# Hybrid decoder layer on one core: the array steps of the state-space heads in three runs per pair, TensorE in the order of the trace, stored halves loaded one pair ahead

## The chip, the cores and the metric

The kernel runs on one core of a Trainium2 chip. The core has five engines that work side by side: TensorE (PE in the profile; PEld is its weight load), VectorE (DVE), ScalarE (ACT), GpSimd (POOL) and SyncE (SP), whose queue issues this kernel's DMAs. The metric is the device time of one execution in microseconds; lower is better. It is 1691.22 us before the change, the median of three runs.

## The reference

One layer of a hybrid decoder, float32, a sequence of 2048 positions, width 1024. The input is normalised and multiplied by one wide matrix; the result feeds two head groups. Group A is a chunked state-space scan with 16 heads of 64, in chunks of 128 positions; group B is a short gated convolution. Both are joined and projected back, normalised, and added to the input. Then a 256-wide embedding is projected, gated and added. Cut to what matters here:

```python
xbc, dt_raw, z_ssd, sc_h, sc_b, sc_c, z_sc = split(rmsnorm(x) @ w_in)
...
# group A, per chunk of 128 positions and per head
cb = einsum("bclgn,bcsgn->bgcls", cc, bc)
y_diag = einsum("bgrcls,bcsgrp->bclgrp", cb[:, :, None] * decay_in, xd)        # outputs
states = einsum("bclgn,bclgrp->bcgrpn", bc, xd * decay_states[..., None])       # states
y_off = einsum("bclgn,bcgrpn->bclgrp", cc, prev_states) * decay_out[..., None]  # offsets
y = y_diag + y_off + d_skip * x
y_ssd = rmsnorm(y * silu(z_ssd))                 # per group of 8 heads
# group B
y_sc = sc_b * causal_dwconv(sc_c * sc_h) * silu(z_sc)
mix = concatenate([y_ssd, y_sc]) @ w_out
x = x + rmsnorm(mix)
return x + sigmoid(x @ w_ple_gate) * (p @ w_ple_proj)
```

## The kernel before

All large products run as three passes of a split type (each operand is cut into a rounded part and a remainder), 128x128 weights against 512 columns at a time. The layer has three stages.

The first stage multiplies the input with the wide matrix (lines 238 to 320, 354 to 750) and writes what the heads need to memory: the convolved values `xs_d`, the gates `gz_d`, the two shared operands `cb_d`, and the running sums of the decay `acs_d`; group B's result goes to `ysc_d`.

The second stage, lines 814 to 1045, is the one that is edited. It handles the sequence in two blocks of 1024 positions (`TB`), each in 8 chunks of 128, and in each block four *pairs*. A pair is two tiles of 128 channels, `j` and `j + 4`, its two *halves* (`gr` 0 and 1), each with two heads (`hh`). That makes eight pairs. Each is written as a set of functions, its *steps*:

- `xs0`, `xs1` (`loads`, L887): the DMA of a half's values into a buffer `xs`; three of these are in use in turn.
- `T0`, `T1` (`transposes`, L891): eight transposes on TensorE into PSUM (`px`), which VectorE scales into `xd` (L903) and `xdd` (L904).
- `load0`, `load1`: DMAs that broadcast decays, `ea` (L911) and the four masks `m` (L946). `decays` (L914) takes the exponent of `ea`; `m00` to `m11` (L948) do so for the masks and multiply them with a shared operand on VectorE (L954).
- `gz0`, `gz1` (L916): the DMA of a half's gates.
- `states` (L920): 32 matmuls `pst` in the profile, a chain of 14 or 16 short operations on VectorE (L938), and two multiplications of `ea` (L941).
- `offsets` (L956): 64 small matmuls `py` (L967) for both halves.
- `out0`, `out1` (`outputs`, L971): 32 matmuls `py` each (L979), then on VectorE the skip and the gate (L982, L983), the store to `yz_d` (L984), the square on ScalarE (L988) and its sum `ssum` (L989). The store reads the buffer that `loads` had filled.

After each block `norms` (L1002) forms the norm of group A from `ssum`: four matmuls `pn` (L226) and a chain through memory. `gs` are two steps at the start of a block (`pg` L867, `pb` L879).

TensorE would have little to do in these steps. The rest of its time goes to the *filler* `under` (L819): the part of the output projection that needs group B alone, 768 matmuls `os` (L838) in 256 *units* of three. Its results go to `part_d`. A list `steps` is written out by hand (L1019 to L1034), and the loop behind it (L1039) runs a step and then as many units as that step's share of the list gives, 22 of them ahead. The list has 127 steps. Near its end the filler also starts `mixes`, which load `yz_d` or `ysc_d` and split it into operands (L792) for the later groups.

This order is only the order in which instructions are traced. The framework then orders each engine's instructions itself, by a priority that follows the trace and by its own estimate of when an operand will be there. On TensorE it so draws filler units ahead of steps, and cuts steps in two. Within an engine the resulting order is fixed; what an instruction has to wait for is a semaphore. A tile's buffer is given to the next tile of its tag when all readers of the old one are done. PSUM has three buffers of two banks for the steps (`pss`) and two banks for the filler (`psm`).

The third stage (L1048 on) does the rest of the output projection, `mo` (called through L210), which adds `part` to it (L1072) to give `x`; then norm, residual, and the gate product `mg`. `out_proj(0)` handles the first two groups of 512 positions, `out_proj(2)` the others. `Loads` (L758) hands out buffers, three per pool; `begin` issues a DMA and `get` returns the tile, after `begin` where that has not been called.

Of the kernel before, what the change touches and what calls it, by code (L numbers as in the profile page):

```python
# [7 lines left out]
F32 = mybir.dt.float32  # L8
# [7 lines left out]
P = 128  # L16
D = 1024
T = 2048
KD = D // P
KM = 2 * KD  # L20
TB = 1024
# [36 lines left out]
def hybrid_kernel(ctx: ExitStack, tc: tile.TileContext, xT, pT, w_t, w_dt, w_o, w_g, w_p, cols_d, cst_d, outT):  # L58
# [47 lines left out]
    class Weights:  # L106
# [4 lines left out]
        def __init__(self, seq):  # L111
            self.seq, self.n, self.ready = seq, 0, []
# [240 lines left out]
    with ExitStack() as st:  # L353
# [373 lines left out]
        for b, prs, order in groups:  # L727
# [16 lines left out]
            if b + 1 < NB:  # L744
# [5 lines left out]
                if n in (6, 7, 8, 9, 10):  # L750
                    next(prep, None)

    pss = ctx.enter_context(tc.tile_pool(name="pss", bufs=3, space=PSUM))
# [58 lines left out]
    with ExitStack() as st:  # L814
# [32 lines left out]
        def heads(b):  # L847
# [34 lines left out]
            def pair(j):  # L882
# [2 lines left out]
                xd, xdd, xs, gz, st = [None, None], [None, None], [None, None], [None, None], {}  # L885

                def loads(gr):  # L887
                    xs[gr] = t4.tile([P, TB], F32, tag="xs", name=f"xs_{b}{jts[gr]}", bufs=3)
                    nc.sync.dma_start(xs[gr], xs_d[b][jts[gr]])

                def transposes(gr):  # L891
                    jt = jts[gr]
                    px = flat(pss.tile([P, 2, TG], F32, tag="ssd", name=f"px_{b}{jt}"))
                    for c in range(NCH):
                        cs = slice(c * CH, (c + 1) * CH)
                        TE.transpose(px[:, cs], xs[gr][:, cs], ident)
                    xd[gr] = t4.tile([P, NCH, P], F32, tag="xd", name=f"xd_{b}{jt}", bufs=3)
                    xdd[gr] = t4.tile([P, NCH, P], F32, tag="xdd", name=f"xdd_{b}{jt}")

                    def bc(a):  # L900
                        return a[:, 2 * jt:2 * jt + 2, :].rearrange("p h c -> p c h").unsqueeze(3).to_broadcast([P, NCH, 2, 64])
                    r4 = lambda a: a.rearrange("p c (h q) -> p c h q", h=2)
                    V.tensor_tensor(r4(xd[gr]), px.rearrange("p (c h q) -> p c h q", c=NCH, h=2), bc(dts[b]), ALU.mult)  # L903
                    V.tensor_tensor(r4(xdd[gr]), r4(xd[gr]), bc(dst[b]), ALU.mult)  # L904
# [106 lines left out]
        for b in range(NB):  # L1011
# [5 lines left out]
        NJ = len(pairs) // NB  # L1017
        both = lambda *fs: lambda: [f() for f in fs]
        p = pairs[0]  # L1019
        steps += [both(begins[0], p["xs0"], p["xs1"], p["load0"], p["load1"]), gs[0][0], gs[0][1], p["T0"],  # L1020
                  both(p["gz0"], p["gz1"]), p["decays"], p["T1"], no, p["m00"], no]
        for n, p in enumerate(pairs):
            b, j = divmod(n, NJ)
            q = pairs[n + 1] if n + 1 < len(pairs) else dict.fromkeys(p, no)
            fresh = j == NJ - 1 and b + 1 < NB
            steps += [both(p["states"], q["xs0"]), p["m01"], p["m10"], p["m11"], p["offsets"], p["out0"]]
            steps += [both(q["load0"], begins[b + 1]) if fresh else q["load0"], q["T0"], both(q["decays"], q["xs1"])]
            if fresh:

                steps += [p["out1"], q["load1"], norms[b], gs[b + 1][0], gs[b + 1][1], both(q["T1"], q["gz0"], q["gz1"]), no,  # L1030
                          q["m00"], no]
            else:
                steps += [p["out1"], both(q["load1"], q["gz0"]), both(q["T1"], q["gz1"]), q["m00"], no]
        steps += [norms[-1]]  # L1034

        filler = under()
        units, lead = 0, 22
# [7 lines left out]
            pass  # L1045


    with ExitStack() as st:  # L1048
        pp = st.enter_context(tc.tile_pool(name="pp", bufs=2))
        L3 = Loads(st, "pl3", 3)  # L1050

        x2s_, ssq_, rs_, sp_ = {}, {}, {}, {}

        def out_proj(t):

            for tg in (t, t + 1):
                x2s_[tg] = [None] * KD
                ssq_[tg] = pp.tile([P, TG], F32, tag="ssq", name=f"ssq2_{tg}")
            for dp in range(0, KD, 2):
                sp = []  # L1060
                for tg in (t, t + 1):
                    x2, ssq = x2s_[tg], ssq_[tg]
                    ps = pss.tile([P, 2, TG], F32, tag="ssd", name=f"mo_{tg}_{dp}")
                    pt = L3.get("part", tg, dp)
                    for i in range(2):
                        for q in range(2):
                            if tg == t:
                                sp.append(W.next(len(sp)))
                            mm3([(ps[:, i, :], sp[2 * i + q], acts_o[tg])], 4 * q, 4, KD)
                        d = dp + i  # L1070
                        x2[d] = pp.tile([P, TG], F32, tag="x2", name=f"x2_{tg}_{d}", bufs=NG * KD)
                        V.tensor_tensor(x2[d], ps[:, i, :], pt[:, i, :], ALU.add)  # L1072
                        if d == 0:
                            S.activation(ssq, x2[d], AF.Square)
                        else:
                            sq = pp.tile([P, TG], F32, tag="sq2", name=f"sq2_{tg}_{d}")
                            S.activation(sq, x2[d], AF.Square)
                            V.tensor_tensor(ssq, ssq, sq, ALU.add)
                        yield

        def norm(tg):

            ps = mm_bank(f"pn2_{tg}")
            TE.matmul(ps, ones_d, ssq_[tg], start=True, stop=True)
            rs = rs_[tg] = pp.tile([P, TG], F32, tag="rs2", name=f"rs2_{tg}")
            S.activation(rs, ps, AF.Sqrt, bias=epsc[:, 0:1])
            V.reciprocal(rs, rs)

        def residual(tg, d):

            x2, xk = x2s_[tg], L3.get("xres", tg, d)
            for i in range(2):
                V.scalar_tensor_tensor(x2[d + i], x2[d + i], col(C_POST + d + i), rs_[tg], ALU.mult, ALU.mult)
                V.tensor_tensor(x2[d + i], x2[d + i], xk[:, i, :], ALU.add)

        def operands(tg, d):

            for i in range(2):
                sp_.setdefault(tg, []).append(split_act(x2s_[tg][d + i], f"x2s_{tg}_{d + i}", FIRST[2 * (tg % 2) + d // 4]))

        def gate(t):

            for dp in range(0, KD, 2):
                sp = []
                for tg in (t, t + 1):
                    banks = pss.tile([P, 2, TG], F32, tag="ssd", name=f"mg_{tg}_{dp}")
                    for i in range(2):
                        d, ts_, ps = dp + i, slice(tg * TG, (tg + 1) * TG), banks[:, i, :]
                        pe = pp.tile([P, TG], F32, tag="pe", name=f"pe_{tg}_{d}")
                        nc.sync.dma_start(pe, ple_d[tg * TG // TB][d, :, tg * TG % TB:tg * TG % TB + TG])  # L1110
                        for q in range(2):
                            if tg == t:
                                sp.append(W.next(len(sp)))
                            mm3([(ps, sp[2 * i + q], sp_[tg])], 4 * q, 4, KD)
                        th = pp.tile([P, TG], F32, tag="gth", name=f"gth_{tg}_{d}")
                        S.activation(th, ps, AF.Tanh, scale=0.5)  # L1116
                        V.scalar_tensor_tensor(th, th, 1.0, pe, ALU.add, ALU.mult)  # L1117
                        V.scalar_tensor_tensor(th, th, 0.5, x2s_[tg][d], ALU.mult, ALU.add)
                        nc.sync.dma_start(outT[d, :, ts_], th)
                        yield  # L1120


        plan = {}

        def after(unit, *steps):
            plan.setdefault(unit, []).extend(steps)

        def second(tg, at_norm, at_res, at_ops):

            after(at_norm, lambda: norm(tg))  # L1130
            for n, u in enumerate(at_res):
                after(u - 1, lambda d=2 * n: L3.begin("xres", tg, d))
                after(u, lambda d=2 * n: residual(tg, d))
            for n, u in enumerate(at_ops):
                after(u, lambda d=2 * n: operands(tg, d))

        def mixes_at(tg, *units):
            m = mixes(tg, 0)
            for n, u in enumerate(units):
                after(u, *m[2 * n:2 * n + 2])  # L1140

        mixes_at(1, -1, -1, 0, 1)
        mixes_at(2, 12, 13, 14, 14)
        mixes_at(3, 15, 15, 16, 17)
        second(0, 16, (19, 20, 21, 22), (29, 29, 30, 30))
        second(1, 18, (24, 25, 26, 27), (31, 31, 32, 32))
        second(2, 32, (35, 36, 37, 38), (45, 45, 46, 46))
        second(3, 34, (40, 41, 42, 43), (47, 47, 48, 48))
        for step in plan.get(-1, ()):
            step()  # L1150
        u = 0
        for stage in (out_proj, gate):
            for t in range(0, NG, 2):
                for _ in stage(t):
                    for step in plan.get(u, ()):
                        step()
                    u += 1
# [62 lines left out]
```

## Time and profile before

| what | us |
|---|---|
| runs | 1688.46, 1693.49, 1691.22 |
| median | 1691.22 |
| the profiled execution's own time | 1696.51 |
| its span, first to last instruction | 1694.8 |
| mean granted clock of TensorE | 0.994 |
| second stage, first to last `os` | 1032.5 to 1318 |
| DMA's share of the second stage's pairs | 0.73 to 0.90 |

Times in the views count from the first instruction. In a row of the timeline stand the start, the length, the engine, the line, the operation, output and inputs by name, the shape and the number of instructions merged; in brackets is the engine's idle time before the row and what ended it. Rows of TensorE overlap a little, as matmuls are pipelined: a duration per matmul is best taken from the starts of two rows. In a row of the waits stand the total, the number of times and the longest. In a row of the groups stand the busy time, the mean in ns of one instruction, and the engine's idle time ahead of them.

### The profile page before, as it was taken

What the parts mean: (1) busy time and instruction counts of PE and PEld (TensorE: products, weight loads), DVE (VectorE), ACT (ScalarE), POOL (GpSimd) and SP (SyncE); (2) the same over time, 40 slices, a digit from 0 to 9 for tenths busy, and PEclk for the clock granted to TensorE, in tenths of its full rate; (3) what the DMA queues carried; (4) which work ended last, traced back from release to release, by engine and by line L of the source; (5) the groups of instructions that cost most, each with busy time, mean ns of one, the idle gap of its engine ahead of it and who ended that gap; (6) DMA issues with size and microseconds to landing.
All of it is one profiled execution on the core that took longest, in us unless ns stands there. A gap on an engine that the chain in (4) does not pass through costs nothing.

```text
span 1694.8 us, 22689 instructions
## 1 busy us (share of the span) xinstructions
PE 1665.9 (98%) x8368; PEld 1360.3 (80%) x8368; DVE 1248.1 (74%) x1837; ACT 780.4 (46%) x1402; POOL 44.8 (3%) x79
## 2 busy tenths in 40 slices
PE   9999999999999999999999999999999899999998
PEld 7888888888888888888888888787777677788886
DVE  6998778988679867778776685779587748878632
ACT  7763544434348434344444364646565324252421
POOL 0000000000000100000000000000000000000000
PEclk9999999999999999999999999999999999999999
DMA  8452322862227322121222248789787735636422
GB/s 299 155 193 81 103 93 89 265 225 106 70 69 248 108 74 100 59 88 67 106 102 83 69 146 267 233 257 293 240 298 229 244 100 168 195 103 211 148 95 87
DMA packets 121539, 261.22 MB, mean 154 GB/s; under 512 B 16970, under 2 KB 18506, under 8 KB 120404
## 3 DMA queue, kind: packets, MB, share of 16 engines
q1 hardware_dynamic: 121428, 259.78, 46.2%
q8 instruction: 65, 1.06, 0.3%
q14 instruction: 46, 0.38, 0.1%
HBM read 191.40 MB, written 68.33 MB: 153 GB/s over the span
## 4 chain that ended last, share of the span: by engine, by line
PE 88%; DMA 4%; DVE 4%; issue 2%; ACT 1%; SPq 0%; POOL 0%; DVEq 0%; POOLq 0%; ACTq 0%
PE mg L210 10%; PE mo L210 8%; PE os L838 6%; PE A_ple L210 3%; PE A_xs1X L306 1%; PE A_gc6X L306 1%; PE A_gc0X L306 1%; PE A_gc7X L306 1%; PE A_gb5X L306 1%; PE A_gb6X L306 1%; PE A_gb2X L306 1%; PE A_z1X L306 1%; PE A_z3X L306 1%; PE A_gc5X L306 1%; PE A_z2X L306 1%
## 5 line engine op out<-in xcount | busy, mean ns | idle before, releaser
L838 PE MATMUL os<-act_m,ws_os 128*128 128x512 f32 x768 | 187.8, 399 | 1.6 <-ACT po L842 0.9
L210 PE MATMUL mo<-act_m,ws_o 128*128 128x512 f32 x768 | 180.8, 396 | 4.5 <-DVE x L1072 4.5
L210 PEld LDWEIGHTS mo<-act_m,ws_o 128*128 128x128 f32 x768 | 144.1, 189 | 42.0 <-issue 6.9
L210 PE MATMUL mg<-act_x2s,ws_g 128*128 128x512 f32 x768 | 176.7, 392 | 0.7 <-ACT gth L1116 0.7
L838 PEld LDWEIGHTS os<-act_m,ws_os 128*128 128x128 f32 x768 | 142.6, 190 | 37.4 <-issue 6.6
L210 PEld LDWEIGHTS mg<-act_x2s,ws_g 128*128 128x128 f32 x768 | 143.1, 188 | 34.1 <-ACT gth L1116 4.4
L135 DVE TENSOR_TENSOR ws_A_gb<-wr_A_gb,ws_A_gb 128x512 fp32r<-128x512 f32 x96 | 65.9, 686 | 34.2 <-ACT ws_A_gb L134 34.2
L134 ACT CAST ws_A_gc<-wr_A_gc 128x512 fp32r<-128x512 f32 x96 | 59.8, 623 | 59.2 <-PE A_gc5X L306 8.3
L134 ACT CAST ws_A_gb<-wr_A_gb 128x512 fp32r<-128x512 f32 x96 | 59.6, 621 | 54.6 <-PE A_gb5Z L306 4.3
L617 DVE SCALAR_TENSOR_TENSOR xo<-ux,cols,xo 128x1024 f32<-128x1024 f32 x60 | 76.6, 1280 | 5.7 <-ACT xo L613 4.6
L951 ACT ACTIVATE m<-m,adt 128x128 f32<-128x128 f32 x256 | 77.4, 392 | 1.6 <-DMA m<-acs_d 1.5
L135 DVE TENSOR_TENSOR ws_A_gc<-wr_A_gc,ws_A_gc 128x512 fp32r<-128x512 f32 x96 | 66.0, 687 | 14.6 <-ACT ws_A_gc L134 13.2
L1117 DVE SCALAR_TENSOR_TENSOR gth<-gth,pe 128x512 f32<-128x512 f32 x32 | 22.1, 690 | 70.4 <-ACT gth L1116 70.3
L1116 ACT ACTIVATE gth<-mg 128x512 f32<-128x512 f32 x32 | 19.1, 598 | 103.7 <-PE mg L210 103.6
L954 DVE SCALAR_TENSOR_TENSOR m<-m,gsb 128x1024 f32<-128x1024 f32 x32 | 39.6, 1246 | 20.4 <-ACT m L951 18.0
L199 ACT CAST act_m<-mraw 128x512 fp32r<-128x512 f32 x64 | 38.0, 620 | 30.3 <-DVE mraw L797 15.4
L210 PE MATMUL A_ple<-act_p,ws_p 128*128 128x512 f32 x192 | 48.1, 408 | 1.9 <-ACT act_p L199 1.5
L134 ACT CAST ws_A_z<-wr_A_z 128x512 fp32r<-128x512 f32 x48 | 29.9, 623 | 42.9 <-DVE wr_A_z L183 11.7
L134 ACT CAST ws_A_xs<-wr_A_xs 128x512 fp32r<-128x512 f32 x48 | 29.9, 623 | 42.5 <-issue 11.6
L135 DVE TENSOR_TENSOR ws_A_z<-wr_A_z,ws_A_z 128x512 fp32r<-128x512 f32 x48 | 32.9, 686 | 21.2 <-ACT ws_A_z L134 21.2
L210 PEld LDWEIGHTS A_ple<-act_p,ws_p 128*128 128x128 f32 x192 | 36.6, 194 | 11.9 <-ACT act_p L199 2.5
L1072 DVE TENSOR_TENSOR x<-mo,part 128x512 f32<-128x512 f32 x32 | 21.9, 684 | 29.0 <-PE mo L210 27.6
(505 smaller groups left out, 3599.8 us busy)
## 6 DMA issues: line engine op xcount, KB each, us to landing
wr_A_gc<-in_w_t_dram SPq DMA_DIRECT2D x64, 256.0 KB, 2.6
wr_A_gb<-in_w_t_dram SPq DMA_DIRECT2D x64, 256.0 KB, 2.7
m<-acs_d SPq DMA_DIRECT2D x32, 512.0 KB, 7.2
ple_d<-A_pe SPq DMA_DIRECT2D x32, 256.0 KB, 3.5
wr_A_xs<-in_w_t_dram SPq DMA_DIRECT2D x32, 256.0 KB, 3.6
ysc_d<-vs SPq DMA_DIRECT2D x16, 512.0 KB, 2.6
wr_A_z<-in_w_t_dram SPq DMA_DIRECT2D x32, 256.0 KB, 2.9
xs_d<-xo SPq DMA_DIRECT2D x16, 512.0 KB, 3.2
```

The costliest lines, as they stand in the source:

```text
L134: S.copy(sp[:, 0, :kn, :], raw[:, :kn, :])
L135: V.tensor_tensor(sp[:, 1, :kn, :], raw[:, :kn, :], sp[:, 0, :kn, :].bitcast(F32), ALU.subtract)
L199: S.copy(a[:, 0, :], src)
L210: TE.matmul(out, sp[:, a, (k0 + k) % 4, :], act[k0 + k][:, b, :], start=k0 + k == 0 and q == 0, stop=k0 + k == n - 1 and q == 2)
L306: TE.matmul(out, sp[:, a, k % 4, :], t[:, b, ts_], start=p in OPENS and k == 0 and q == 0, stop=k == nk - 1 and q == 2, skip_group_check=True)
L617: V.scalar_tensor_tensor(o, u[:, q:q + TB], col(w0 + q), o, ALU.mult, ALU.add)
L838: TE.matmul(ps, sp[:, a, k, :], acts_o[tg][KD + kk][:, b_, :], start=kk == 0 and n == 0, stop=kk == KD - 1 and n == 2)
L951: S.activation(m[:, c, :], m[:, c, :], AF.Exp, bias=nacs[b][:, h, c:c + 1])
L954: V.scalar_tensor_tensor(mf, mf, 1.0, s["gsb"][gr], ALU.min, ALU.mult)
L1072: V.tensor_tensor(x2[d], ps[:, i, :], pt[:, i, :], ALU.add)
L1116: S.activation(th, ps, AF.Tanh, scale=0.5)
L1117: V.scalar_tensor_tensor(th, th, 1.0, pe, ALU.add, ALU.mult)
```

## The change

Five edits. TensorE is wrapped from the start of the second stage to its end: each of its instructions gets an ordering edge on the one traced before, which adds no semaphore but holds the framework to the order of the trace. The list of steps is written anew, with 117 steps: a pair's TensorE work now stands in three steps, `states`, then `offsets` with both outputs, then both transposes of the next pair; an empty step stands ahead of the second of them. Both loads of the next pair's `xs` are in the `states` step. `xs` has four buffers in place of three, and `xd` two in place of three. At the list's end two more empty steps stand ahead of the last norm. In `out_proj(0)` the `part` tile of the next product is loaded one product ahead.

```diff
+    class InOrder:
+        def __init__(self, engine):
+            self.engine, self.last = engine, None
+        def __getattr__(self, name):
+            f = getattr(self.engine, name)
+            def call(*a, **k):
+                inst = f(*a, **k)
+                if self.last is not None:
+                    tc.add_manual_dep(inst.ins, self.last.ins.name, NOSYNC, reason="in the order of the trace")
+                self.last = inst
+                return inst
+            return call
+    TE = InOrder(TE)
...
-                    xs[gr] = t4.tile([P, TB], F32, tag="xs", name=f"xs_{b}{jts[gr]}", bufs=3)
+                    xs[gr] = t4.tile([P, TB], F32, tag="xs", name=f"xs_{b}{jts[gr]}", bufs=4)
...
-                    xd[gr] = t4.tile([P, NCH, P], F32, tag="xd", name=f"xd_{b}{jt}", bufs=3)
+                    xd[gr] = t4.tile([P, NCH, P], F32, tag="xd", name=f"xd_{b}{jt}")
...
-        steps += [both(begins[0], p["xs0"], p["xs1"], p["load0"], p["load1"]), gs[0][0], gs[0][1], p["T0"],
-                  both(p["gz0"], p["gz1"]), p["decays"], p["T1"], no, p["m00"], no]
+        steps += [both(begins[0], p["xs0"], p["xs1"], p["load0"], p["load1"]), gs[0][0], gs[0][1], both(p["T0"], p["T1"]),
+                  both(p["gz0"], p["gz1"]), p["decays"], p["m00"], no]
         for n, p in enumerate(pairs):
...
-            steps += [both(p["states"], q["xs0"]), p["m01"], p["m10"], p["m11"], p["offsets"], p["out0"]]
-            steps += [both(q["load0"], begins[b + 1]) if fresh else q["load0"], q["T0"], both(q["decays"], q["xs1"])]
+            steps += [both(p["states"], q["xs0"], q["xs1"]), p["m01"], p["m10"], p["m11"], no,
+                      both(p["offsets"], p["out0"], p["out1"]), both(q["load0"], begins[b + 1]) if fresh else q["load0"],
+                      both(q["T0"], q["T1"], q["decays"])]
             if fresh:
-                steps += [p["out1"], q["load1"], norms[b], gs[b + 1][0], gs[b + 1][1], both(q["T1"], q["gz0"], q["gz1"]), no,
-                          q["m00"], no]
+                steps += [q["load1"], norms[b], no, gs[b + 1][0], gs[b + 1][1], both(q["gz0"], q["gz1"]), q["m00"]]
             else:
-                steps += [p["out1"], both(q["load1"], q["gz0"]), both(q["T1"], q["gz1"]), q["m00"], no]
-        steps += [norms[-1]]
+                steps += [both(q["load1"], q["gz0"]), q["gz1"], q["m00"], no, no]
+        steps += [no, no, norms[-1]]
...
+    TE = nc.tensor
...
                     pt = L3.get("part", tg, dp)
+                    if t == 0:
+                        L3.begin("part", *((t + 1, dp) if tg == t else (t, dp + 2) if dp < KD - 2 else (t + 2, 0)))
...
+        L3.begin("part", 0, 0)
         mixes_at(1, -1, -1, 0, 1)
```

`q` is the next pair, `fresh` the last pair of the first block, and `no` an empty step.

## The prediction

> **What bounds the kernel now.** The page comes first: engines, then the waits of TensorE (PE) in order of their total.
>
> ```profile
> PE 1665.9 (98%) x8368; PEld 1360.3 (80%) x8368; DVE 1248.1 (74%) x1837; ACT 780.4 (46%) x1402; POOL 44.8 (3%) x79
> ```
> ```profile
> PE pn L226 <- DVE ssum L989: 6.4, 3, 3.6
> PE px L896 <- DMA xs<-xs_d: 6.1, 3, 2.7
> PE mo L210 <- DVE x L1072: 4.5, 4, 2.2
> ```
>
> PE is busy for 98% of the span, so a gain has to come out of its idle time or out of what it does slowly while busy. The first two waits lie in the stage of the heads, the stage that the change edits; the third lies behind it. The timeline of PE in that stage shows where they fall and what surrounds them:
>
> ```profile
> 1229.87 1.07 PE L896 MATMUL px<-cst,xs 128*128 128x128 f32 x8 [2.53 <-DMA xs<-xs_d]
> 1262.14 1.06 PE L896 MATMUL px<-cst,xs 128*128 128x128 f32 x8 [0.82 <-DMA xs<-xs_d]
> 1295.58 1.84 PE L896 MATMUL px<-cst,xs 128*128 128x128 f32 x8 [2.73 <-DMA xs<-xs_d]
> ...
> 1187.41 1.05 PE L226 MATMUL pn<-ssum,ones_d 128*32 128x512 f32 x4 [1.85 <-DVE ssum L989]
> ...
> 1317.17 0.96 PE L838 MATMUL os<-act_m,ws_os 128*128 128x512 f32 x3
> 1321.70 1.05 PE L226 MATMUL pn<-ssum,ones_d 128*32 128x512 f32 x4 [3.56 <-DVE ssum L989]
> ...
> 1325.09 1.92 PE L226 MATMUL pn<-ssum,ones_d 128*32 128x512 f32 x4 [1.03 <-DVE ssum L989]
> ```
>
> Eight transposes took 1.06 at one place and 1.84 at another. The windows view tells why; a row has the stretch and its length, the busy time of PE, its weight loads, VectorE (DVE), ScalarE (ACT) and GpSimd, then the granted clock, the DMA share and GB/s:
>
> ```profile
> 1182.00:1190.00 8.00, 6.15 (x27) 4.04 (x26) 2.13 (x3) 6.11 (x13) 0.00 (x0) 1.00 0.90 305
> 1230.80:1234.30 3.50, 3.50 (x11) 2.56 (x10) 3.30 (x4) 3.50 (x11) 0.00 (x0) 0.51 1.00 375
> 1295.60:1299.10 3.50, 3.50 (x13) 2.65 (x14) 2.32 (x3) 3.50 (x11) 0.00 (x0) 0.52 1.01 358
> 1322.60:1330.00 7.40, 6.37 (x17) 3.25 (x16) 6.17 (x10) 2.68 (x4) 0.00 (x0) 0.54 0.59 194
> ```
>
> After the idle times of 2.53, 2.73 and 3.56 us the clock was about half for 3.5, 3.5 and 7.4 us; after the 1.85 us at 1187 it stayed at 1.00. A long wait is therefore paid for again: (1 - 0.51) x 3.5 + (1 - 0.52) x 3.5 = 3.4 us for the loads, (1 - 0.54) x 7.4 = 3.4 us for the norm. The Trainium skill, "TensorE: Matmul & The Clock Gate", section "Why this matters for your kernels", asks only that idle gaps of over some 3 us be avoided; by it the two waits of 2.53 and 2.73 us would have cost no clock, and the sum below would be 3.4 us smaller. The rows show half clock behind both, so the measurement decides.
>
> **What the change removes.** (a) *Loads of xs.* At present a pair's second half is loaded into one of three buffers, and SyncE's queue stands until the store of an older half has landed:
>
> ```profile
> SPq L889 <- DMA yz_d<-xs: 32.3, 11, 6.7
> ```
>
> With four buffers and both loads issued at the states step of the pair before, each load takes the buffer of a pair whose stores are long gone. This also frees what stood behind it on the same queue: yz stores, mask loads, gate loads. The loads then have a whole pair before them. The px waits go: 6.1 us, and 3.4 us of clock. Cutting xd from three buffers to two costs nothing, as the new T0 and T1 come behind both outputs that read the old pair.
>
> (b) *The last norm.* PE had one unit of filler (x3, a k-step of "os") left between the last outputs and the norm. In the new list ten steps lie between them, and a step is followed by 234/116 = 2.02 units (117 steps instead of 127, 22 of the 256 units ahead). The price of a matmul of 128x512 comes from an undisturbed stretch, start to start:
>
> ```profile
> 1026.26 2.88 PE L306 MATMUL A_gc7X<-act_A,ws_A_gc 128*128 128x512 f32 x12
> 1028.98 2.88 PE L306 MATMUL A_gb7X<-act_A,ws_A_gb 128*128 128x512 f32 x12
> ```
>
> That is 2.72/12 = 0.227 us, 0.68 us a unit, so about 20 units or 13.7 us cover the norm's input. At present the sums needed from the end of the outputs at about 1317.2 until about 1325.1, 7.9 us. The cover is long enough: 3.56 + 1.03 = 4.6 us and 3.4 us of clock go. If it were not, they would stay.
>
> (c) *Visits to the array.* PE leaves the filler for the small matmuls and comes back; here is how one pair's steps are split:
>
> ```profile
> 1093.64 0.43 PE L924 MATMUL pst<-xdd,btok 128*64 128x128 f32 x2
> 1094.01 2.79 PE L838 MATMUL os<-act_m,ws_os 128*128 128x512 f32 x11
> 1096.72 1.96 PE L924 MATMUL pst<-xdd,btok 128*64 128x128 f32 x30
> 1098.61 5.73 PE L838 MATMUL os<-act_m,ws_os 128*128 128x512 f32 x24
> 1104.28 0.44 PE L967 MATMUL py<-ea,sprev 64*64 64x128 f32 x4
> 1104.64 0.96 PE L838 MATMUL os<-act_m,ws_os 128*128 128x512 f32 x3
> 1105.53 1.96 PE L967 MATMUL py<-ea,sprev 64*64 64x128 f32 x60
> 1107.43 1.97 PE L979 MATMUL py<-m,xd 128*64 128x128 f32 x32
> ...
> 1109.66 1.03 PE L896 MATMUL px<-cst,xs 128*128 128x128 f32 x8
> 1110.45 3.01 PE L838 MATMUL os<-act_m,ws_os 128*128 128x512 f32 x12
> 1113.39 1.97 PE L979 MATMUL py<-m,xd 128*64 128x128 f32 x32
> ```
>
> From 1104.28 to 1107.43 are 3.15 us for 64 offsets and 3 fillers. Sixty offsets took 1.90, so 64 take 2.03; the fillers take 0.68; 0.44 us is the price of one visit more. For the split states it is 0.37 + 2.71 - 2 x 0.063 - 11 x 0.227 = 0.46 us. The second output's own visit shows 2.94 - 12 x 0.227 = 0.22 us on its way in, and I put it at 0.3. Now a pair has up to three visits beyond those of the new order: states split in two in 7 of 8 pairs, offsets split in all 8, the second output apart in 7. With PE held to the order of the trace and the outputs put together, 15 x 0.45 + 7 x 0.3 = 8.8 us go; by the cheapest row 22 x 0.22 = 4.8, by the dearest 22 x 0.46 = 10.1.
>
> Removed in sum: 6.1 + 3.4 + 4.6 + 3.4 + 8.8 = 26.3 us. I count nothing for the wait of 1.85 us at the middle norm, since PE comes there only four steps and two transposes after the outputs (8 units, 5.5 us, and 1.6 us), less than the 7.9 us above; it may go or grow to some 4. I count nothing for the earlier "part" loads: the 4.5 us of "mo" wait for DVE, not for a load by name, and of them only this one lies well inside the half of "mo" that the edit touches:
>
> ```profile
> 1357.87 55.99 PE L210 MATMUL mo<-act_m,ws_o 128*128 128x512 f32 x242 [1.23 <-DVE x L1072]
> ```
>
> At most these 1.2 us could go; the number of loads on SyncE's queue stays the same.
>
> **What it adds.** PE can no longer draw filler ahead of a step that is not ready, so every late input is now idle PE, with all the filler queued behind it. Three steps matter; the DVE durations are from the groups of 1065 to 1320 us:
>
> ```profile
> L954 DVE SCALAR_TENSOR_TENSOR m<-m,gsb 128x1024 f32<-128x1024 f32 x30 | 37.2, 1248 | 19.9 <-ACT m L951 17.5 <-POOL gsb L872 1.3 <-issue 0.9
> L938 DVE SCALAR_TENSOR_TENSOR sprev<-sprev,ea,pst 128x64 f32<-128x64 f32 x112 | 22.2, 274 | 4.9 <-issue 4.0 <-PE pst L924 0.9
> L982 DVE SCALAR_TENSOR_TENSOR xs<-xs,ds,py 128x1024 f32<-128x1024 f32 x16 | 20.4, 1277 | 17.2 <-PE py L979 17.1
> L941 DVE SCALAR_TENSOR_TENSOR ea<-ct,ea 128x1024 f32<-128x1024 f32 x16 | 18.8, 1218 | 0.0
> L983 DVE TENSOR_TENSOR xs<-xs,gz 128x1024 f32<-128x1024 f32 x15 | 18.3, 1218 | 0.1
> L903 DVE TENSOR_TENSOR xd<-px,dts 128x1024 f32<-128x1024 f32 x14 | 17.1, 1219 | 3.5 <-PE px L896 3.4
> L904 DVE TENSOR_TENSOR xdd<-xd,dst 128x1024 f32<-128x1024 f32 x14 | 17.1, 1218 | 0.1
> ...
> L989 DVE TENSOR_TENSOR ssum<-ssum,gz 128x1024 f32<-128x1024 f32 x10 | 12.2, 1222 | 9.6 <-ACT gz L988 9.5
> ```
>
> *States* wait for both halves' xd and xdd. From the first output's end to the states step lie 1.9 us of the second output, 4 units, two rows of transposes of 0.8 (1109.66 to 1110.45), and 12 units: about 14.4 us. DVE has in it two times L982, L983, L989 (1.28 + 1.22 + 1.22) and four tensor products of 1.22, together 12.3 us, and perhaps a mask (1.25) and a weight split. It just fits. *Offsets* wait for 14 or 16 steps of L938 (2.8 to 3.2 us) and two of L941 (2.4), 5.5 us, before them 10 units, 6.9 us; one interposed mask still fits. *Transposes* wait for a PSUM buffer freed by L982; covered by 4 units. So an ordinary pair waits about nothing. But DVE is nearly full in the two stretches in which the mixing operands for the later groups are made as well:
>
> ```profile
> 1127.80:1160.40 32.60, 32.60 (x271) 26.29 (x270) 28.97 (x46) 22.15 (x53) 0.20 (x1) 1.00 0.84 268
> 1160.40:1200.60 40.20, 37.52 (x316) 28.58 (x315) 30.00 (x45) 27.03 (x64) 2.75 (x3) 1.00 0.90 297
> ```
>
> PE's own time for a new pair is 13 x 2.02 units (17.9 us), 1.6 of transposes, 1.9 of states, 2.0 of offsets, 3.8 of outputs and about 0.9 of visits, 28.1 us; DVE's 28.97 us in the first of these rows is more. I take 5 us of new waits for the whole stage (bounds 0, if DVE's order suits, and 20, at 2.5 us a pair).
>
> *The start of "mo".* The operands of the first group are split into buffers that "os" frees at unit 240 of 256, which in the new list comes behind the last outputs; 16 units and the norm, 12 us, are then left until "mo" asks for them. At present all but the one unit at 1317 runs ahead of those outputs, and the waits of the norm give more time still. DVE has the outputs' sums (7.4 us) and 16 operations of about 0.7 us in that time and in the 5 us in which "mo" takes them one by one. 3 us, between 0 and 8.
>
> Behind this, "mo" and "mg" keep PE busy to the end, so what the heads gain reaches the end: 26.3 - 5 - 3 = 18.3 us. The profiled execution took 1696.5 us (span 1694.8), which becomes 1678.2; it was 5.3 us above the median of the runs, 1691.2, so the forecast for the median is **1673**.
>
> **Rivals.**
> *1. DVE sets the pace.* Each pair waits 1 us more than I counted and "mo" takes its full 8 us: 18.3 - 8 - 5 = 5.3 us are left, 1686. For it speak the two DVE rows just shown; against it that DVE waits in the same groups, 17.1 us for PE's outputs and 17.5 for ScalarE's masks.
> *2. Slower: the order turns late operands into long idle times.* The place is the states step. If DVE puts the sums (L989, which wait for ScalarE) or the masks ahead of xdd, xdd comes 2.5 us late; by the rows at 1230 and 1295 such an idle time costs 1.7 us of clock more, 4.2 us a pair, 33.6 us in all against 26.3 removed: 1698.5. It decides from about 3.3 us a pair on. Against it stands that this needs the same lateness in all eight pairs. The Trainium skill, same page, section "Part 3: Packing small matmuls", has matmuls start and end strictly in their order, so that nothing behind a late one can pass it; no row quoted here shows it otherwise.
> *3. No new waits.* SyncE's queue, freed of its 32.3 us, brings masks and gates earlier, nothing waits: 26.3 us, with the middle norm and one "mo" wait up to 29.4: 1662 to 1665.
> That the edit does nothing is hardly possible: four buffers and the new list change the program whatever the order.
>
> **How the numbers follow.** A measurement of this kernel tells about 0.3% (5 us) from no change. Forecast 0.52 (1666 to 1681), rival 1 0.18, rival 2 0.10, rival 3 0.20. Rival 1 lies across the border at 1686.1, 0.08 of it faster and 0.10 the same; hence faster 0.80, same 0.10, slower 0.10. The range goes from 1660, below rival 3, to 1690, the greater part of rival 1; beyond it are rival 2 and the rest of rival 1.
>
> **What would show it.** Right: no px wait for DMA xs; one row each of x32 pst, x64 py L967, x64 L979 and x16 px per pair; no pn wait at the end; clock 1.00 from 1040 us to the end of the heads; the heads some 20 us shorter. Wrong: new PE waits on pst for xdd, on py for ea or m of over 2.5 us with clock near 0.5 behind them, or "mo" waiting for act_m by more than 8 us; or DVE busy over 95% of a pair's window.

## The result and the profile after

The changed kernel takes 1679.16 us (median of 6 runs, 1675.72 to 1683.07) where the kernel before takes 1691.76 (6 runs): ratio 0.9923, 95% interval 0.9901 to 0.9945, 12.6 us less. The forecast was 1673 in a range from 1660 to 1690. The profiled execution took 1683.07 us, its span is 1681.2 against 1694.8. Two of the twelve runs of one version below, edges and loads together on the old list, were in a slower state and are left out of its time.

The timeline of TensorE after the change, one pair in the middle and the end of the heads (in this kernel all matmuls of the heads stand under L763, the wrapper's line):

```profile
1092.09 1.97 PE L763 MATMUL pst<-xdd,btok 128*64 128x128 f32 x32
1093.99 7.09 PE L763 MATMUL os<-act_m,ws_os 128*128 128x512 f32 x30
1101.01 1.98 PE L763 MATMUL py<-ea,sprev 64*64 64x128 f32 x64
1102.92 3.71 PE L763 MATMUL py<-m,xd 128*64 128x128 f32 x64
1106.56 3.02 PE L763 MATMUL os<-act_m,ws_os 128*128 128x512 f32 x12
1109.42 1.91 PE L763 MATMUL px<-cst,xs 128*128 128x128 f32 x16
...
1293.46 13.90 PE L763 MATMUL os<-act_m,ws_os 128*128 128x512 f32 x60
1307.29 1.07 PE L763 MATMUL pn<-ssum,ones_d 128*32 128x512 f32 x8
...
1309.78 5.61 PE L210 MATMUL mo<-act_m,ws_o 128*128 128x512 f32 x24
```

States, offsets, both outputs and both transposes are one row each; in other pairs a row is split only where TensorE waited inside it. Before, the same work was cut into seven to nine rows in each pair but the last. In the heads TensorE has 118 rows before and 77 after, and it leaves the filler for a step 41 times before and 31 after. Twenty units of filler (x60) stand ahead of the last norm, and nothing waits there. The waits of TensorE after:

```profile
PE pst L763 <- DVE xdd L924: 3.7, 3, 2.4
PE mo L210 <- DVE x L1096: 3.5, 4, 1.3
PE os L763 <- ACT po L862: 2.4, 2, 1.8
PE py L763 <- DVE m L974: 2.4, 1, 2.4
...
PE mo L210 <- ACT act_m L199: 1.8, 1, 1.8
PE py L763 <- DVE ea L961: 1.2, 3, 0.4
...
PE mo L210 <- DVE act_m L200: 0.8, 1, 0.8
```

Both waits that the change was read to remove are gone: px for the loads (6.1 us) and pn for the norm (6.4 us, the middle norm's 1.85 among them). New ones stand in their place. The longer of them in the timeline, and the granted clock behind them (third figure from the end of a row of the windows view):

```profile
1164.22 2.76 PE L763 MATMUL py<-m,xd 128*64 128x128 f32 x30 [2.35 <-DVE m L974]
...
1247.23 0.41 PE L763 MATMUL pst<-xdd,btok 128*64 128x128 f32 x2 [1.12 <-DVE xdd L924]
1250.01 3.25 PE L763 MATMUL pst<-xdd,btok 128*64 128x128 f32 x30 [2.37 <-DVE xdd L924]
...
1317.14 0.50 PE L210 MATMUL mo<-act_m,ws_o 128*128 128x512 f32 x1 [1.75 <-ACT act_m L199]
```
```profile
1165.20:1168.60 3.40, 3.40 (x21) 2.78 (x17) 3.40 (x4) 2.10 (x3) 0.00 (x0) 0.51 0.86 194
1250.50:1253.90 3.40, 3.40 (x28) 2.98 (x25) 3.07 (x7) 3.40 (x13) 0.00 (x0) 0.50 1.04 423
1318.80:1322.20 3.40, 3.40 (x9) 2.19 (x7) 2.72 (x5) 1.32 (x2) 0.00 (x0) 0.51 0.54 161
```

Each of the three is followed by 3.4 us at half clock, about 1.7 us more; between the third and its stretch lies one more wait, of 0.78 us. So the heads, from the first os to the row from which mo runs on (1326.94 before, 1309.78 after), went from 294.4 to 277.4 us, 17.0 less; mo and what follows went from 367.9 to 371.4, 3.5 more, of which 0.7 are three matmuls of mo that stood between the norm's rows before.

### The profile page after: what moved, and what is told of

Its sections match the earlier page's. It is cut to its first block, busy times and chain, and to the rows that moved or that the text cites. A ratio compares the mean times of both kernels' runs of the same rounds, so it can differ in the third digit from the quotient of the medians.

```text
span 1681.2 us, 22694 instructions
## 1 busy us (share of the span) xinstructions
PE 1655.4 (98%) x8368; PEld 1358.9 (81%) x8368; DVE 1247.7 (74%) x1837; ACT 779.9 (46%) x1402; POOL 49.0 (3%) x79
## 4 chain that ended last, share of the span: by engine, by line
PE 86%; DMA 6%; DVE 4%; ACT 2%; issue 1%; SPq 1%; DVEq 0%; ACTq 0%
PE mg L210 10%; PE mo L210 8%; PE os L763 4%; PE A_ple L210 3%; DMA mraw<-yz_d 2%; PE py L763 1%; DMA ea<-acs_d 1%; PE A_xs1X L306 1%; PE A_gc6X L306 1%; PE A_gc0X L306 1%; PE A_gb5X L306 1%; PE A_gc7X L306 1%; PE A_gb6X L306 1%; PE A_z3X L306 1%; PE A_xs3X L306 1%; PE A_gc5X L306 1%
## 5 line engine op out<-in xcount | busy, mean ns | idle before, releaser
L763 PE MATMUL os<-act_m,ws_os 128*128 128x512 f32 x768 | 184.8, 396 | 3.1 <-ACT po L862 2.4
L763 PEld LDWEIGHTS os<-act_m,ws_os 128*128 128x128 f32 x768 | 142.5, 189 | 37.8 <-issue 4.7
L135 DVE TENSOR_TENSOR ws_A_gc<-wr_A_gc,ws_A_gc 128x512 fp32r<-128x512 f32 x96 | 66.1, 688 | 14.6 <-ACT ws_A_gc L134 13.3
L974 DVE SCALAR_TENSOR_TENSOR m<-m,gsb 128x1024 f32<-128x1024 f32 x32 | 39.1, 1247 | 16.3 <-ACT m L971 14.6
L134 ACT CAST ws_A_z<-wr_A_z 128x512 fp32r<-128x512 f32 x48 | 29.9, 622 | 42.7 <-DVE wr_A_z L183 10.8
L200 DVE TENSOR_TENSOR act_m<-mraw,act_m 128x512 fp32r<-128x512 f32 x64 | 41.7, 685 | 6.7 <-ACT act_m L199 6.6
```

The source lines that it names most:

```text
L134: S.copy(sp[:, 0, :kn, :], raw[:, :kn, :])
L135: V.tensor_tensor(sp[:, 1, :kn, :], raw[:, :kn, :], sp[:, 0, :kn, :].bitcast(F32), ALU.subtract)
L200: V.tensor_tensor(a[:, 1, :], src, a[:, 0, :].bitcast(F32), ALU.subtract)
L763: inst = f(*a, **k)
L974: V.scalar_tensor_tensor(mf, mf, 1.0, s["gsb"][gr], ALU.min, ALU.mult)
```

## The experiments

Ratios are to the kernel before, timed beside each version, with 95% intervals. The first three take the change apart.

**The loads alone**, on the old list and with the framework free to order:

```diff
-                    xs[gr] = t4.tile([P, TB], F32, tag="xs", name=f"xs_{b}{jts[gr]}", bufs=3)
+                    xs[gr] = t4.tile([P, TB], F32, tag="xs", name=f"xs_{b}{jts[gr]}", bufs=4)
...
-                    xd[gr] = t4.tile([P, NCH, P], F32, tag="xd", name=f"xd_{b}{jt}", bufs=3)
+                    xd[gr] = t4.tile([P, NCH, P], F32, tag="xd", name=f"xd_{b}{jt}")
...
-            steps += [both(p["states"], q["xs0"]), p["m01"], p["m10"], p["m11"], p["offsets"], p["out0"]]
-            steps += [both(q["load0"], begins[b + 1]) if fresh else q["load0"], q["T0"], both(q["decays"], q["xs1"])]
+            steps += [both(p["states"], q["xs0"], q["xs1"]), p["m01"], p["m10"], p["m11"], p["offsets"], p["out0"]]
+            steps += [both(q["load0"], begins[b + 1]) if fresh else q["load0"], q["T0"], q["decays"]]
```

> The kernel before with the loads alone changed: four xs buffers, two xd buffers, both loads of the next pair in the states step; old list, framework free to order. Theory (three separate sources: loads 9.5 us, last norm 8 us, visits 9 us, less new waits): the px waits on DMA xs (6.1 us) and the half clock behind two of them (3.4 us) go, pn waits of 6.4 us and the split visits stay (about 118 runs of one kind on TensorE in the heads); 9.5 us faster than before, some 1682. Rival A (the loads carry it all, order and list are idle): 12 to 13 us faster, 1679. Rival B (order and list carry it, loads were hidden): within 3 us of before.

1687.47 us, ratio 0.9976 (0.9962 to 0.999): 4 us, less than half of 9.5. No px wait on a load is left and only 0.7 us of pn, but one wait of 6.6 us stands in a new place. First VectorE, then TensorE, both from this kernel's timeline:

```profile
1234.60 1.28 DVE L982 SCALAR_TENSOR_TENSOR xs<-xs,ds,py 128x1024 f32<-128x1024 f32 x1 [0.94 <-PE py L979]
1244.70 0.75 DVE L797 SCALAR_TENSOR_TENSOR mraw<-mraw,cols,gn 128x512 f32<-128x512 f32 x1 [8.82 <-DMA mraw<-yz_d]
```
```profile
1257.72 3.25 PE L924 MATMUL pst<-xdd,btok 128*64 128x128 f32 x30 [6.58 <-DVE xdd L904]
```

VectorE stood 8.8 us for the load of a mixing operand (L797) that is needed only some 70 us later at mo. The framework had drawn it ahead of the pair's own gates and xdd: its place in the list is unit 240 of the filler's 256 or later, and 197 had run. Behind it all of these came late. The clock was half from 1253.6 to 1260.4; 4.1 us of this lie in the wait itself, so it cost 1.3 us more. Rival A falls by the time. Rival B's 3 us lie within the interval (1.7 to 6.4 us); it falls by the trace, as the px waits of 6.1 us are gone. The theory's sum falls twice: this wait and its clock took 7.9 us back, and 5.7 us of pn waits that were to stay went, as 30 matmuls of filler now stood between the last outputs and the last norm.

**The list without the ordering edges**, that is the changed kernel less the wrapper:

```diff
-    TE = InOrder(TE)
```

> The changed kernel without the ordering edges on TensorE; list, loads and part tiles as changed. Theory: the framework draws filler ahead again, so visits come back (about 9 us) and the filler before the last norm is used up early (pn waits of some 4 us and half clock behind), while the new waits of the ordered kernel (pst, py and po 9.7 us, clock 3.4 us) shrink; in all 1680 to 1686, at most even with the changed kernel. Rival A (loads carry all): 1679. Rival C (the list alone does it and the edges only cost): 1670 or less, since 13 us of new waits are gone and the visits stay few.

1675.17 us, ratio 0.99 (0.9878 to 0.9922). The theory is wrong here: visits did not come back.

```profile
1090.85 1.97 PE L943 MATMUL pst<-xdd,btok 128*64 128x128 f32 x32
1092.75 7.10 PE L857 MATMUL os<-act_m,ws_os 128*128 128x512 f32 x30
1099.77 1.98 PE L986 MATMUL py<-ea,sprev 64*64 64x128 f32 x64
1101.68 3.71 PE L998 MATMUL py<-m,xd 128*64 128x128 f32 x64
```

This is the changed kernel's pattern, with no edge that holds it: 77 rows of TensorE in the heads here too, and 60 filler matmuls still ahead of the last norm. Why the framework now leaves the order of the list nearly alone, no view shows. Its waits in the heads are 5.0 us in place of 9.7, but its interval overlaps that of the changed kernel, so that the edges cost something is not shown.

**The ordering edges alone**, on the kernel before:

```diff
+    TE = InOrder(TE)
...
+    TE = nc.tensor
     with ExitStack() as st:
         pp = st.enter_context(tc.tile_pool(name="pp", bufs=2))
```

> The kernel before with the ordering edges on TensorE alone; old list and old loads. Theory: 32 visits instead of 38, worth about 2.5 us; but filler can no longer cover the late xs loads, so px waits stay at 6 us or grow, with half clock behind them, and the last norm has 9 units (6.4 us) where its sums took 7.9 us; within 5 us of before, 1687 to 1697. Rival (the order alone makes the gain): 1683 or less.

```profile
PE px L765 <- DMA xs<-xs_d: 14.9, 6, 7.9
```

1698.9 us, ratio 1.0046 (1.0029 to 1.0062): slower, 2 us beyond the theory's bound of 1697. The px waits grew from 6.1 to 14.9 us, as filler cannot be drawn ahead of them. The last norm, though, waited 0.16 us behind 30 matmuls of filler (7.0 us); the list's longer cover is not the only thing that can save it. **Edges and loads together on the old list**, the two diffs for the kernel before joined, leave only the list to tell from the changed kernel (and the part tiles, below):

> The kernel before with the loads ahead (four xs buffers, two xd) and the ordering edges on TensorE, on the old list. Against the changed kernel only the list (and part) is undone. Theory: no px wait on xs any more, 32 visits to the array in place of 16, so 16 x 0.4 = 6 us slower than the changed kernel, and 1 to 3 us of pn waits since the last norm has 9 units; 1684 to 1690. Rival (the list brings nothing once loads and order are there): 1677 to 1681.

1691.41 us, ratio 0.9992 (0.9981 to 1.0004), beyond the theory's 1690. The list is worth some 12 us where 7 to 9 were expected: beside the visits there are longer waits than in the changed kernel, the middle norm's (pn) above all.

```profile
PE pn L765 <- DVE ssum L1009: 6.2, 1, 6.2
PE pst L765 <- DVE xdd L924: 5.7, 3, 3.4
PE py L765 <- DVE ea L961: 3.5, 4, 2.3
```

**The loads undone in the changed kernel:**

```diff
-                    xs[gr] = t4.tile([P, TB], F32, tag="xs", name=f"xs_{b}{jts[gr]}", bufs=4)
+                    xs[gr] = t4.tile([P, TB], F32, tag="xs", name=f"xs_{b}{jts[gr]}", bufs=3)
...
-            steps += [both(p["states"], q["xs0"], q["xs1"]), p["m01"], p["m10"], p["m11"], no,
+            steps += [both(p["states"], q["xs0"]), p["m01"], p["m10"], p["m11"], no,
...
-                      both(p["offsets"], p["out0"], p["out1"]), both(q["load0"], begins[b + 1]) if fresh else q["load0"],
+                      both(p["offsets"], p["out0"], p["out1"]), both(q["load0"], q["xs1"], begins[b + 1]) if fresh else both(q["load0"], q["xs1"]),
```

> The changed kernel with the loads undone: three xs buffers, the first half's load in the states step, the second half's in the step of the next pair's masks. Theory (few visits need the loads ahead): both transposes now wait for a load that waits for a store, 2 to 5 us a pair with half clock behind the longer ones; 15 to 40 us slower than the changed kernel, 1694 to 1720, slower than the kernel before. Rival (the loads are hidden by the filler between): within 4 us of 1679.

```profile
PE px L763 <- DMA xs<-xs_d: 56.1, 6, 10.2
```

1746.02 us, ratio 1.032 (1.03 to 1.0339), more than the 1720 expected. `xd` keeps its two buffers here. Loads alone bring 4 us, but the list cannot stand without them: the two transposes of a pair are now one step, and the second one's load is issued only behind the stores of the pair before. In the second pair the stores issue from 1079.24 on, the next load of `xs` at 1084.11, and TensorE, which was done with the first transposes at about 1082, stands until 1090.71.

**The price of a visit.** In the changed kernel the second half's outputs come one step later:

```diff
-                      both(p["offsets"], p["out0"], p["out1"]), both(q["load0"], begins[b + 1]) if fresh else q["load0"],
+                      both(p["offsets"], p["out0"]), both(p["out1"], q["load0"], begins[b + 1]) if fresh else both(p["out1"], q["load0"]),
```

> The changed kernel with the second half's outputs moved two filler units later, so that every pair has one visit to the array more; all else as changed. Theory (a visit costs 0.22 to 0.46 us): 8 visits cost 1.8 to 3.7 us, seen in the timeline as about 0.3 us per filler group between the two outputs; 1681 to 1683, though the later second output gives its masks 1.4 us more, which can take back the one wait on m of 2.4 us. Rival (a visit costs nothing, the heads got shorter by fewer waits alone): 1679 or less and filler groups of 6 between the outputs take 6 x 0.227 us from the outputs' last matmul on.

```profile
1260.66 1.97 PE L763 MATMUL py<-m,xd 128*64 128x128 f32 x32
1262.55 1.66 PE L763 MATMUL os<-act_m,ws_os 128*128 128x512 f32 x6
1264.15 1.97 PE L763 MATMUL py<-m,xd 128*64 128x128 f32 x32
1266.04 1.66 PE L763 MATMUL os<-act_m,ws_os 128*128 128x512 f32 x6
```

Six fillers take 1.60 us in place of 6 x 0.227 = 1.36, and the two outputs 1.89 + 1.89 in place of 3.64 (1102.92 to 1106.56 above): 0.38 us a visit, 3.0 us for eight. The time was 1681.76, ratio 0.9937 (0.9918 to 0.9956), 2.6 us over the changed kernel; the two intervals overlap, so the price rests on the timeline. The Trainium skill, "TensorEngine Tiling (Array Packing)", section "Key Properties", says that a change of tiling mode drains the array; the rows agree, and no run here separates the drain from the rest of the restart.

**The mixing operand.** In the changed kernel the first group's L817 may not stand ahead of the seventh pair's gated outputs on VectorE (`gated` holds the instruction of L1003, the last of each pair):

```diff
+                if tg == 0:
+                    tc.add_manual_dep(inst.ins, gated[6].ins.name, NOSYNC, reason="not ahead of the seventh pair")
```

In the changed kernel VectorE's timeline shows what the loads' own experiment showed, the instruction at 1248.73 being the one that PE awaits at 1250.01:

```profile
1230.65 1.28 DVE L1002 SCALAR_TENSOR_TENSOR xs<-xs,ds,py 128x1024 f32<-128x1024 f32 x1 [1.12 <-PE py L763]
1238.22 0.75 DVE L817 SCALAR_TENSOR_TENSOR mraw<-mraw,cols,gn 128x512 f32<-128x512 f32 x1 [6.29 <-DMA mraw<-yz_d]
...
1248.73 1.22 DVE L924 TENSOR_TENSOR xdd<-xd,dst 128x1024 f32<-128x1024 f32 x1
```

> The changed kernel with one edge more: the first group's mixing operands (L817) may not stand ahead of the seventh pair's gated outputs on VectorE. Theory: the pst waits of 1.1 and 2.4 us at 1247 to 1250 and the half clock behind them (1.7 us) come from VectorE standing 6.3 us for the DMA of such an operand; they go, 4 to 5 us, unless the operands now come later at the start of mo (2.6 us of waits there), which may grow by up to 5; 1674 to 1679. Rival (VectorE is simply full in that pair): the pst waits stay above 2.5 us and the time stays at 1679 or above.

1671.86 us, ratio 0.9883 (0.9866 to 0.99). No pst wait is left, and mo's waits for act_m fell from 2.6 to 0.7 us; the gain of 7 us is over the 4 to 5 expected. Of the 7.0 us that the heads lost, 5.2 are the wait in this pair (1.12 and 2.37) and its half clock (1.7); 1.3 are a wait of the filler in the first pair (1.81 before, 0.50 now), which the edge does not touch. **The same edge without the ordering edges:**

> The changed kernel without the ordering edges on TensorE and with the same edge on the mixing operands. Theory: the version without ordering edges had no long stall in the heads (its mixing operand stood 4 us at most), so there is little left to gain: 1673 to 1677, no pst wait above 1 us. Rival (the mixing operand is the remaining cost of this version too): 1671 or less.

1671.22 us, ratio 0.9873 (0.9854 to 0.9892), between the theory's 1673 and the rival's 1671. The two versions are alike: once the operand is held back, the ordering edges neither cost nor bring anything that can be measured. These two have the lowest times of all versions.

**The cover of the last norm**, six steps in place of ten:

```diff
-        steps += [no, no, norms[-1]]
+        steps = steps[:-2] + [norms[-1], no, no]
```

> The changed kernel with the last norm six steps behind the last outputs in place of ten (12.3 filler units, 8.4 us, in place of 13.7 us). Theory: the norm's sums needed 10.8 us from the end of the outputs in the changed kernel, 3 us of them a wait of VectorE for an operand's load, so PE waits 0.5 to 2.5 us for pn; the start of mo gets its operands 3 us earlier and loses its act_m waits of 2.6 us and the half clock behind (1.7 us); 1676 to 1679. Rival (the start of mo is bound by the chain of loads whatever the place of the outputs): act_m waits stay at 2 us or more and the time rises to 1680 to 1683.

1679.78 us, ratio 0.9923 (0.9908 to 0.9938), just over the theory's 1676 to 1679.

```profile
1302.28 1.05 PE L763 MATMUL pn<-ssum,ones_d 128*32 128x512 f32 x4
1305.28 1.05 PE L763 MATMUL pn<-ssum,ones_d 128*32 128x512 f32 x4 [1.95 <-DVE ssum L1009]
...
1312.06 29.62 PE L210 MATMUL mo<-act_m,ws_o 128*128 128x512 f32 x129
```

A wait of 1.95 us came at the norm, and mo starts without a wait for act_m, as the theory has it; the middle norm, which the edit does not touch, waited 2.9 us in this kernel. One wait went and others came, at no gain.

**The part tiles** back at their point of use:

```diff
-                    if t == 0:
-                        L3.begin("part", *((t + 1, dp) if tg == t else (t, dp + 2) if dp < KD - 2 else (t + 2, 0)))
...
-        L3.begin("part", 0, 0)
```

> The changed kernel without the part tiles loaded one product ahead. Theory (mo waits for VectorE, which stands for mixing operands, not for part): within 2 us of the changed kernel, 1677 to 1681, mo waits on x of 3 to 5 us in both. Rival (the part tiles were late): mo waits on x rise by 3 us or more, 1682 or above.

1679.13 us, ratio 0.9915 (0.9898 to 0.9933): no difference from the changed kernel that can be measured, and mo waits 3.5 us on x in both.

**The masks.** On the version with the held operand and without ordering edges, the second half's mask loads issued with the first half's:

```diff
-both(q["load0"], begins[b + 1]) if fresh else q["load0"],
+both(q["load0"], q["load1"], begins[b + 1]) if fresh else both(q["load0"], q["load1"]),
...
-                steps += [q["load1"], norms[b], no, gs[b + 1][0], gs[b + 1][1], both(q["gz0"], q["gz1"]), q["m00"]]
+                steps += [no, norms[b], no, gs[b + 1][0], gs[b + 1][1], both(q["gz0"], q["gz1"]), q["m00"]]
...
-                steps += [both(q["load1"], q["gz0"]), q["gz1"], q["m00"], no, no]
+                steps += [q["gz0"], q["gz1"], q["m00"], no, no]
```

> The version without ordering edges and with the edge on the mixing operands (1671), and the second half's mask loads issued with the first half's. Theory: the one wait on m of 2.7 us in the fourth pair, with half clock behind (1.7 us), comes from the mask loads that stand late on SyncE's queue; it goes, 2 to 4 us, 1667 to 1670. Rival (ScalarE's casts for the later groups hold the masks up, not their loads): the wait stays above 2 us, 1670 to 1673.

```profile
1161.83 1.93 PE L1001 MATMUL py<-m,xd 128*64 128x128 f32 x30 [2.47 <-DVE m L976]
```
```profile
1150.00:1172.00 22.00, 19.53 (x196) 15.76 (x194) 20.54 (x35) 15.07 (x35) 1.19 (x1) 1.00 0.90 269
```

1673.79 us, ratio 0.9889 (0.9872 to 0.9907): no gain, and the wait stays, so the theory of late mask loads falls. VectorE is busy for 20.5 of 22 us around it. In the fourth pair casts and splits for the later groups share both engines with the masks; that these are the cause was argued from the timeline and not tried.

## Why the prediction was right, and where its sizes were off

*Loads and last norm.* Both went as worked out: no px wait for a load, no pn wait, no half clock behind them. The cover of 13.7 us was needed more than I said: six steps, 8.4 us, were too few, since the sums took 10.8 us from the end of the outputs in place of 7.9; for 3.0 of these VectorE stood for another mixing operand. The clock that I added for the norm was 0.5 us too much: in the stretch of 7.4 us TensorE was busy for 6.37, and the rest was the wait of 1.03 already counted. That the middle norm's 1.85 us went too was luck: in the version without the part tiles and the one with six steps ahead of the last norm, whose edits leave its place as it is, it waited 1.1 and 2.9 us.

*Visits.* The forecast was 8.8 us. The heads lost 17.0 us. Of the waits in them 14.6 went (6.1, 6.4, and four small ones of 0.9, 0.5, 0.4 and 0.3, which I had left out of the sum) and 4.9 of clock (3.4 for the loads, and 1.5 of the norm's: TensorE was busy for 3.31 us at 0.55 up to 1326.94); 9.7 (3.7, 2.4, 2.4, 1.2) and 3.4 of clock came; three matmuls are 0.7. That leaves 17.0 - 14.6 - 4.9 + 9.7 + 3.4 - 0.7 = 9.9 us for the visits. This is what is left over and not a count: by 0.38 us each it would be 26 visits, where I had counted 22 and TensorE leaves the filler only 10 times less. The 22 hold cuts of another kind too. In four pairs of the kernel before it was transposes alone that cut the offsets in two:

```profile
1208.48 0.44 PE L967 MATMUL py<-ea,sprev 64*64 64x128 f32 x4
1208.85 0.77 PE L896 MATMUL px<-cst,xs 128*128 128x128 f32 x5
1209.55 1.96 PE L967 MATMUL py<-ea,sprev 64*64 64x128 f32 x60
1211.44 1.97 PE L979 MATMUL py<-m,xd 128*64 128x128 f32 x32
```

From 1208.48 to 1211.44 are 2.96 us; in the changed kernel's rows 64 offsets take 1.91 and 5 transposes 5 x 0.104 = 0.52, so such a cut cost 0.5 us as well. And what removed the visits was named wrongly in part: "with PE held to the order of the trace" was not needed; the list and the early loads do it alone.

*New waits: the term that was mis-sized.* I had 5 us in the heads and 3 at mo, without clock. In the heads 9.7 us of waits and 3.4 us of clock came, 13.1; at mo the waits rose from 4.5 to 6.1 us, with about as much half clock as before, which leaves some 1 us of its 3.5 unexplained. The states step was named as the place, and for 5.2 of the 13.1 it was; the cause was another than the full VectorE that I argued from. It was an instruction of a later stage that stood, waiting for its load, ahead of the pair's own work on VectorE. Holding it back gave 7 us, and the time came to 1672, next to the forecast's 1673. The wait for a mask in the fourth pair, 4.1 us with its clock, stays without a cause that was tried. I had counted the mixing operands as work of VectorE and at the start of mo, not as something that VectorE waits for in the heads, though its timeline of the kernel before has four of them at 1246 us; there their loads were merely in time:

```profile
1245.99 2.77 DVE L797 SCALAR_TENSOR_TENSOR mraw<-mraw,cols,gn 128x512 f32<-128x512 f32 x4
```

*Signs.* Of what was to show it right, the px and pn waits went. The clock was not 1.00 to the end of the heads (0.51 and 0.50 in the windows at 1165 and 1250), and the heads lost 17.0 us, not some 20. The new waits of 2.35 and 2.37 us, with half clock behind them, stayed just under the 2.5 us that was to show it wrong. That the time fell within the range with new waits of more than twice the size owes something to the middle norm and the four small waits, 4.0 us that were not counted on.

*Rivals.* Rival 2 was the mechanism of the edges alone, at px in place of states: 1.0046. Rival 1's mark, over 95% of a pair's window on VectorE, was not reached: in the windows view of the changed kernel, the stretch with the wait for m and the one with the long pst waits have it busy (third pair of figures) for 86% each.

```profile
1150.76:1190.87 40.11, 37.76 (x320) 30.25 (x318) 34.45 (x51) 32.63 (x80) 3.20 (x3) 0.96 0.93 311
1235.13:1268.96 33.83, 29.74 (x255) 24.62 (x254) 29.10 (x40) 18.03 (x43) 0.29 (x1) 0.95 0.82 259
```

Rival 3 did not come either: the heads of the changed kernel have 9.7 us of new waits, and even the version with the held operand keeps 4.5 and takes 1672 where the rival had 1662 to 1665.

## What to carry to other kernels

Putting small array steps together pays some 0.4 us a visit here, but only if every operand of the joined step is there; the early load is worth little by itself and the list is a loss without it. After each change of an order, look on the in-order engines for instructions of a later stage that moved ahead and wait there for a DMA: in two versions VectorE stood so for 6 and 9 us, and in the changed kernel an ordering edge on the instructions of that group gave 7 us back, where the change itself had brought 12.6.

## What the runs showed of the hardware

Whether an idle time halves the clock is not told by its length alone. In the changed kernel 2.35 us were followed by 3.4 us at 0.51; in the kernel with the masks 2.47 us at the same place were not (clock 1.00 over the whole window above). The Trainium skill, "TensorE: Matmul & The Clock Gate", Part 1, has an activity window of some 3.4 us that runs freely. The same idle time could then fill more or less of one window; these two runs and the length of the half-clock stretches agree with that, and no run here shows the window itself. A wait of about 2 to 3 us in this kernel has thus to be priced with a chance of 1.7 us more.
